# A two-layer encoder on one core: loads at the end of the recurrence move from SyncE's queue to GpSimd's

## The chip, the cores and the metric

One of the eight cores of a Trainium2 chip runs the whole program. The metric is the device time of one execution in microseconds; the time of a kernel is the median of several runs. Engines are called by name: TensorE (PE in the profile; PEld is its weight load), VectorE (DVE), ScalarE (ACT), GpSimd (POOL) and SyncE (SP). SyncE computes nothing: it issues transfers. ScalarE and GpSimd can issue transfers as well, from their own queues, between their own instructions. Each queue is worked off in order.

## The reference, cut to what matters

The model is a trunk of two layers on 768 tokens, two sequences of 512 and 256 that share the weights. In layer 0 two mixers run side by side on the normalised input, four heads of differential attention and eight heads of a bidirectional RWKV-7 recurrence, and share an output projection:

```python
st = (st * w_t[:, :, None, :] + sa[..., None] * (kk_t * a_t)[:, :, None, :]
      + v_t[..., None] * k_t[:, :, None, :])
y = jnp.einsum('bhvk,bhk->bhv', st, r_t)
...
y = ((y - mean) * lax.rsqrt(var + RWKV_GN_EPS)).reshape(B, S, H * N) * lnx_w + lnx_b
return ((y + bonus.reshape(B, S, H * N)) * g).astype(xn.dtype)
...
return jnp.concatenate([out_a.astype(xn.dtype), out_b], axis=-1) @ w_out0
```

Layer 1 is dilated window attention in three groups. Each layer ends with a SwiGLU feed-forward of width 2816, and each part has an RMS norm before and behind it. All is float32.

## The kernel before, in words

Tokens are worked on in six tiles of 128. Products with weights run in three passes: a weight or an activation is cast to a rounded upper half by ScalarE, the lower half is the difference, taken by VectorE or GpSimd (`split`, lines 137 to 140), and upper times upper, upper times lower and lower times upper are added. A weight matrix comes in blocks of 512 KB: `raw` (lines 132 to 135) takes one of two buffers `wraw` and issues its load from SyncE, `weights` splits it. The lower halves of the output projection `wo0` are taken by GpSimd.

The recurrence is worked in chunks of 64 tokens, twelve forward and twelve backward, in alternation (`rwkv`, from line 916). For each chunk `fetch` and `fetch_inverse` (lines 938 to 956) load seven pieces from device memory, all from SyncE's queue: KB, two halves of RH, AL, two halves of the values into SUV, and the inverse Ti. They are fetched three chunks ahead. RH, AL, SUV and Ti have four buffers, KB three. `prep` makes the products that need no state and `chain` does the step itself, with copies by ScalarE and VectorE between its small products. When both directions have passed both chunks of a tile, `finish` (line 1029 on) ends it: it loads the tile's values into `gz` (line 1036), which has one buffer, takes mean and variance on VectorE with a square on ScalarE into `gq`, a power on GpSimd (lines 156 and 157), then loads the tile's gate into `gq`, one buffer shared with the square (line 1044), multiplies and adds on VectorE (lines 1045 to 1050), and has TensorE transpose the result, which is split into the operand of the output projection. Two tiles end at the sixth step of the twelve, two at the eighth and two at the last.

The rounds of the recurrence are written in three parts. The first five run beside the differential attention. Then come the sixth to the ninth, after them the four raw loads of the attention's rows `o` and the eight blocks of `wo0`, and then the last three. Behind them the output projection runs over the tiles (`outproj`), each tile followed by its post-norm (`postnorm`, lines 224 to 236), which needs `mix_post` and the tile's row `x`, both loaded by SyncE into space that the recurrence gives free. The projection takes five banks in turn for its half tiles, and the post-norm frees them. Before the last two tiles `ahead` loads the first two blocks of `gate0` with `raw` and the first of `up0` with SyncE. Then the feed-forward of layer 0 starts.

The order of instructions on each engine is not the order of the program: a planner simulates time, with priorities. Rounds have a raised priority, `prep` a lowered one, and float32r products the lowest, so that they fill gaps. The program order of the loads thus says only what they depend on.

Of the kernel before, what the change touches and what calls it, by code (L numbers as in the profile page):

```python
# [18 lines left out]
P = 128  # L19
# [35 lines left out]
class Core:  # L55
# [3 lines left out]
    def __init__(self, ctx, tc, A):  # L59
        self.tc, self.nc, self.A, self.ctx = tc, tc.nc, A, ctx  # L60
        nc = self.nc
        self.n, self.half, self.turn, self.last = 0, 0, 0, None
        self.qk, self.dq, self.dv, self.banks = {}, {}, {}, {}
        self.const = ctx.enter_context(self.pool("const"))
        self.sm = ctx.enter_context(self.pool("sm", bufs=6))
        self.mh = self.const.tile([P, 8], F32, tag="mh", name="mh")
        nc.gpsimd.memset(self.mh, -0.5)
        nc.scalar.activation(out=self.small("warm", 8, 1), in_=self.mh, func=AF.Square)
# [62 lines left out]

    def raw(self, src, w=1024):
        r = self.wp.tile([P, 1024], F32, tag="wraw", name=self.uid("wraw"), bufs=self.rb)
        self.nc.sync.dma_start(r[:, :w], src)
        return r

    def split(self, hi, lo, x, eng=None):
# [164 lines left out]

    def ffn(self, L, X, hp, post, end, ready):

# [8 lines left out]
        def up(ms):  # L313
# [7 lines left out]
            def product(W, x):  # L321
                o = three(self.bank(UP)[:, 0:H])
                for k in range(4):
                    ws = slice(k * P, (k + 1) * P)
                    for j, (w, a) in enumerate(((0, 0), (0, 1), (1, 0))):
                        self.mm(o, W[w][:, ws], x[a](k), k == 0 and j == 0, k == 3 and j == 2)
                return o

            def add(o, x, b, eng=nc.vector):
                eng.tensor_tensor(out=o, in0=x, in1=b, op=ALU.add)  # L330

            def run(n):
# [8 lines left out]
                def result(i, j, f, *a):  # L341
                    o = sv[:, i, j]
                    if n == 0:
                        f(o, *a)
                        nc.scalar.activation(out=o, in_=o, func=AF.Silu)
                    else:
                        f(a[0], *a)
                        nc.gpsimd.tensor_tensor(out=o, in0=o, in1=a[0], op=ALU.mult)  # L348
                v1 = vec("v1", 2)
                nc.scalar.copy(out=v1, in_=product(next(W), X["B11"]))  # L350
                yield
                p2 = product(next(W), X["B21"])
                yield
                p4 = product(next(W), X["T4"])
                u1, u2, v5 = vec("u1"), vec("u2"), vec("v5")
                add(u1, v1, product(next(W), X["T2"]))
                result(0, 0, add, v1, p2)
                nc.scalar.copy(out=v5, in_=product(next(W), X["T1"]))
                add(u2, u1, product(next(W), X["T3"]))
# [556 lines left out]
    def rwkv(self, rw, park, out):  # L916

        nc, A = self.nc, self.A
        am = []
        for d in "fb":  # L920
            t = rw.tile([P, P], I32, tag="am" + d, name="am" + d)
# [107 lines left out]
        def finish(t):  # L1029

            y = ys[:, t]
            hv = lambda x: x.rearrange("p (h v) -> p h v", h=8)
            bc = lambda x: x.unsqueeze(2).to_broadcast([P, 8, 64])
            st = tile("gst", [P, 3, 8], 2)
            z, q = (tile(n, [P, 512]) for n in ("gz", "gq"))
            nc.sync.dma_start(z, park["v"][t * P:(t + 1) * P])
            nc.vector.tensor_reduce(out=st[:, 0], in_=hv(y), axis=AX.X, op=ALU.add)
            nc.vector.tensor_scalar(out=st[:, 0], in0=st[:, 0], scalar1=1.0 / 64, scalar2=None, op0=ALU.mult)
            nc.vector.tensor_tensor(out=hv(y), in0=hv(y), in1=bc(st[:, 0]), op=ALU.subtract)
            nc.scalar.activation(out=q, in_=y, func=AF.Square)  # L1040
            nc.vector.tensor_reduce(out=st[:, 1], in_=hv(q), axis=AX.X, op=ALU.add)
            self.rpow(st[:, 2], st[:, 1], 1.0 / 64, 64e-5)
            g = tile("gq", [P, 512])
            nc.sync.dma_start(g, park["g"][t])
            nc.vector.tensor_tensor(out=hv(z), in0=hv(z), in1=bc(self.bon[:, t]), op=ALU.mult)
            nc.vector.tensor_tensor(out=z, in0=z, in1=lb, op=ALU.add)
            nc.vector.tensor_tensor(out=hv(y), in0=hv(y), in1=bc(st[:, 2]), op=ALU.mult)
            nc.vector.tensor_tensor(out=y, in0=y, in1=lw, op=ALU.mult)
            nc.vector.tensor_tensor(out=z, in0=y, in1=z, op=ALU.add)
            nc.vector.tensor_tensor(out=z, in0=z, in1=g, op=ALU.mult)  # L1050
            b = self.bank("tr")
            for j in range(4):
                self.tr(b[:, j * P:(j + 1) * P], z[:, j * P:(j + 1) * P])
            out(t, b)
# [264 lines left out]
def body(ctx, tc, A):  # L1319
    nc = tc.nc  # L1320
    C = Core(ctx, tc, A)
    dp = ctx.enter_context(tc.tile_pool(name="dp", bufs=1, space=DRAM, reuse_waits="tile"))
    park = {}
# [64 lines left out]
    def wo(L, n, pool):  # L1388

        def slot(i):  # L1390
            return None if i < C.wb else [pool.tile([P, 1024], F32R, tag=f"{x}{i}", name=C.uid(x)) for x in ("xwh", "xwl")]
        return [C.weights(A[f"wo{L}"][i], slot=slot(i), eng=None if L else nc.gpsimd) for i in range(n)]
    extra = ExitStack()
    rounds(SW, SO)
    for j in range(4):
        C.split(xh[:, j], xl[:, j], C.raw(park["o"][j], T)[:, :T])
# [5 lines left out]
    def wides(L, pool):  # L1402
        return C.wide(pool, f"mix_post{L}", "wpost"), C.wide(pool, f"ffn_pre{L}", "wpre")

    def out_and_norm(L, src, Ws, ks, wide=None):

        sides[0] = ExitStack()
        raw = sides[0].enter_context(C.pool(f"r3{L}", side="right")).tile([P, D], F32, tag="r3", name=C.uid("r3"))
        xp = sides[0].enter_context(C.pool(f"xt{L}", side="right"))
        xt = [[xp.tile([P, 4, T // 2], F32R, tag=f"T{i}{n}", name=C.uid("T")) for n in "hl"] for i in range(3)]  # L1410
        with C.phase(f"ho{L}") as hp:
            C.tmp, C.bw = hp, D
            xs = [hp.tile([P, D], F32, tag="x", name=C.uid("x"), bufs=3) for t in range(NT)]
            wq, wr = wide or wides(L, hp)
            for t in range(NT):
                nc.sync.dma_start(xs[t], src[t])

            def done(t, ms):
                C.postnorm(ms, wq, xs[t])
                nc.sync.dma_start(park["x"][t], xs[t])  # L1420
                C.prenorm(t, xs[t], wr, xh, xl, tags=NORM, xt=xt)
            ready = []
            C.outproj(xh, xl, done, lambda: ready.extend(C.ahead(L, raw)), Ws, ks)
        extra.close()
        return operands(xt), ready
# [11 lines left out]
    def ffn(L, X, ready):  # L1437
        with C.phase(f"hf{L}") as hp:
            w, xs = {}, {}

            def fetch(t, eng):
                xs[t] = C.tmp.tile([P, D], F32, tag="xr", name=C.uid("xr"), bufs=4)
                eng.dma_start(xs[t], park["x"][t])

            def end():
                sides[0].close()
                sides[0] = ExitStack()
                C.tmp, C.bw = sides[0].enter_context(C.pool(f"end{L}", side="right")), D
                w["q"] = C.wide(C.tmp, f"ffn_post{L}", "wpost")
                if L == 0:  # L1450
                    w["r"] = C.wide(C.tmp, "mix_pre1", "wpre")

            def post(t, m):
                if t == 0:
                    for i in range(4):
                        fetch(i, nc.sync)
                x = xs[t]
                C.postnorm(m, w["q"], x, halves=L == 1 and t == NT - 1)
                if L == 1 and t == NT - 1:
                    nc.sync.dma_start(A["y"][t, :, 0:512], x[:, 0:512])  # L1460
                    nc.scalar.dma_start(A["y"][t, :, 512:D], x[:, 512:D])
                elif L == 1:
                    nc.sync.dma_start(A["y"][t], x)
                else:
                    nc.gpsimd.dma_start(park["x"][t], x)
                    if t:
                        C.prenorm(t - 1, xs[t - 1], w["r"], xh, xl, tags=("sc", "ob"))
                    if t == NT - 1:
                        C.prenorm(t, x, w["r"], xh, xl, tags=("sc", "ob"))
                if 1 <= t <= 2:  # L1470
                    fetch(t + 3, nc.sync if L else nc.gpsimd)
            C.ffn(L, X, hp, post, end, ready)
        sides[0].close()

    X = out_and_norm(0, A["x"], W, range(8))
    ffn(0, *X)
    extra = ExitStack()
    xw = extra.enter_context(C.pool("xw1"))
# [155 lines left out]
```

## Time and profile before

| | |
|---|---|
| median of 3 runs | 2126.71 us (2123.24 to 2132.2) |
| the profiled execution | 2126.21 us, span 2124.4 us |
| TensorE busy | 2048.7 us, 96% of the span |
| VectorE, ScalarE, GpSimd busy | 65%, 43%, 42% of the span |
| issues of SyncE's queue (q1) | 168.00 MB, 25.4% of the transfer engines' time |
| issues of ScalarE's (q10) and GpSimd's (q0) | 12.03 MB and 6.83 MB |
| mean granted clock of TensorE | 0.973 of full |

The span runs from the first to the last instruction. In the lists of instructions the columns are the start and the duration in us, the engine, the line of the kernel, the operation, what it writes and reads, how many were merged, and in brackets the idle time of the engine before it and what ended that. A q behind an engine's name marks its queue, as for an issue of a transfer. A stretch of time is given in us from the span's start.

### The profile page before, as it was taken

Reading aid. Unit: us, or ns where it says so; the run is one execution under the profiler, and the core shown is the slowest. Engines: PE = TensorE matmul, PEld = TensorE weight load, DVE = VectorE, ACT = ScalarE, POOL = GpSimd, SP = SyncE. Lnnn points to the kernel's source line nnn. Section 1 sums busy time; section 2 is a strip of 40 time slices with the busy share of each in tenths; the row PEclk is TensorE's granted clock in tenths of the full one; section 3 lists DMA queues with packets and bytes.
Section 4 is the critical chain, followed back from the end, with each engine's and each line's share of the span. In section 5 each row is a group of like instructions: output and inputs, shape, how many; then the busy total and the mean of one; then the engine's idle time right before and its main releaser. Section 6 shows DMA issues by size and latency. Waiting matters only on the chain. (4 is left out here: it accounts for less than half of the span.)

```text
span 2124.4 us, 33739 instructions
## 1 busy us (share of the span) xinstructions
PE 2048.7 (96%) x13270; PEld 1772.5 (83%) x13270; DVE 1378.2 (65%) x2147; ACT 905.9 (43%) x1703; POOL 886.5 (42%) x833
## 2 busy tenths in 40 slices
PE   7999999999998989999999999999998999999998
PEld 7767776777887778999999998888677999999997
DVE  5456996856579566566666657543568566666665
ACT  5467555447554254433333335222444433333332
POOL 4344341653113156543444535443137544543442
PEclk9999997999999999999999999999999999999999
DMA  4334434114365311211222235221131222221124
GB/s 156 87 75 90 97 74 137 55 26 144 84 184 161 129 64 61 80 60 60 73 77 70 72 137 193 74 71 38 51 109 60 71 79 70 70 69 60 60 80 149
DMA packets 150227, 189.01 MB, mean 89 GB/s; under 512 B 95926, under 2 KB 107784, under 8 KB 150068
## 3 DMA queue, kind: packets, MB, share of 16 engines
q1 hardware_dynamic: 126880, 168.00, 25.4%
q10 hardware_dynamic: 20372, 12.03, 2.0%
q0 software_dynamic: 2816, 6.83, 1.0%
q8 instruction: 104, 1.70, 0.3%
q14 instruction: 55, 0.45, 0.1%
HBM read 150.20 MB, written 36.23 MB: 88 GB/s over the span
## 5 line engine op out<-in xcount | busy, mean ns | idle before, releaser
L83 PE MATMUL gm<-xh,w 128*128 128x384 f32 x896 | 249.1, 342 | 2.8 <-ACT xh L139 2.8
L140 DVE TENSOR_TENSOR wl<-wraw,wh 128x1024 fp32r<-128x1024 f32 (+1 forms) x96 | 126.0, 1313 | 151.7 <-ACT wh L139 150.3
L83 PE MATMUL gm<-T,w 128*128 128x384 f32 x1032 | 203.6, 340 | 7.9 <-ACT w L139 7.3
L83 PE MATMUL gm<-xh,wh 128*128 128x256 f32 (+3 forms) x640 | 208.8, 348 | 0.8 <-ACT pad L489 0.8
L83 PE MATMUL gm<-xl,wh 128*128 128x256 f32 (+3 forms) x640 | 207.6, 348 | 0.0
L83 PE MATMUL gm<-xh,wl 128*128 128x256 f32 (+3 forms) x640 | 206.1, 346 | 0.0
L140 DVE TENSOR_TENSOR w<-S,w 128x512 fp32r<-128x512 f32 x176 | 168.8, 961 | 43.8 <-ACT w L139 36.4
L83 PEld LDWEIGHTS gm<-T,w 128*128 128x128 f32 x1032 | 184.1, 188 | 12.7 <-ACT w L139 8.5
L139 ACT CAST wh<-wraw 128x1024 fp32r<-128x1024 f32 (+1 forms) x103 | 107.5, 1046 | 163.8 <-PE gm L83 96.8
L139 ACT CAST w<-S 128x512 fp32r<-128x512 f32 x176 | 108.9, 621 | 156.7 <-POOL S L291 54.6
L83 PEld LDWEIGHTS gm<-xh,w 128*128 128x128 f32 x896 | 167.3, 192 | 7.7 <-ACT xh L139 3.6
L139 ACT CAST w<-wraw 128x512 fp32r<-128x512 f32 x126 | 76.0, 620 | 206.7 <-PE gm L83 138.1
L83 PE MATMUL gm<-xl,w 128*128 128x384 f32 x448 | 153.4, 342 | 3.0 <-DVE xl L140 3.0
L293 POOL TENSOR_TENSOR S<-wraw,S 128x512 f32<-128x512 f32 x42 | 62.8, 1496 | 204.8 <-DVE w L140 204.8
L140 DVE TENSOR_TENSOR w<-wraw,w 128x512 fp32r<-128x512 f32 x126 | 117.5, 949 | 38.1 <-ACT w L139 37.9
L83 PE MATMUL sc<-xh,w 128*128 128x384 f32 x512 | 140.8, 336 | 1.0 <-DVE u L330 1.0
L83 PEld LDWEIGHTS gm<-xh,wh 128*128 128x128 f32 (+1 forms) x640 | 120.2, 194 | 21.8 <-issue 5.8
L83 PEld LDWEIGHTS gm<-xh,wl 128*128 128x128 f32 (+1 forms) x640 | 119.9, 194 | 20.6 <-issue 7.0
L83 PEld LDWEIGHTS gm<-xl,wh 128*128 128x128 f32 (+1 forms) x640 | 120.0, 194 | 19.7 <-issue 7.3
L392 DVE TENSOR_TENSOR acc<-acc,ob 128x512 f32<-128x512 f32 x128 | 87.4, 683 | 66.6 <-PE ob L83 65.5
L83 PE MATMUL sc<-T,w 128*128 128x384 f32 x552 | 111.2, 340 | 7.4 <-ACT v L350 3.3
L348 POOL TENSOR_TENSOR sil<-sil,v 128x384 f32<-128x384 f32 x44 | 46.9, 1066 | 163.1 <-DVE v L330 162.9
(502 smaller groups left out, 5301.5 us busy)
## 6 DMA issues: line engine op xcount, KB each, us to landing
wraw<-in_gate SPq DMA_DIRECT2D x44, 512.0 KB, 3.4
wraw<-in_down SPq DMA_DIRECT2D x44, 512.0 KB, 3.7
wraw<-in_up SPq DMA_DIRECT2D x40, 512.0 KB, 3.5
wraw<-in_wqk SPq DMA_DIRECT2D x20, 512.0 KB, 3.7
wraw<-in_wo SPq DMA_DIRECT2D x14, 512.0 KB, 4.0
wraw<-in_wrkv SPq DMA_DIRECT2D x12, 512.0 KB, 3.5
KB<-pkKB SPq DMA_DIRECT2D x24, 256.0 KB, 3.2
pkx<-x SPq DMA_DIRECT2D x12, 512.0 KB, 3.4
```

Source lines behind the costliest of these rows:

```text
L83: return self.nc.tensor.matmul(o, a, b, start=start, stop=stop)
L139: self.nc.scalar.copy(out=hi, in_=x)
L140: (eng or self.nc.vector).tensor_tensor(out=lo, in0=x, in1=hi.bitcast(F32), op=ALU.subtract)
L293: eng.tensor_tensor(out=s2, in0=a12, in1=s2, op=ALU.subtract)
L348: nc.gpsimd.tensor_tensor(out=o, in0=o, in1=a[0], op=ALU.mult)
L392: nc.vector.tensor_tensor(out=accs[t][:, fs], in0=accs[t][:, fs], in1=os[t, f], op=ALU.add)
```

## The change

`raw` issues its load from `self.rq`. That is SyncE's queue, but from line 1394, between the fifth and the sixth round of the recurrence, to the feed-forward of layer 0, as the program is written, it is GpSimd's. The two loads of each tile end are issued by GpSimd always. The loads that `fetch`, `fetch_inverse`, `wides`, the rows of `x` and the direct load of `up0` issue stay with SyncE.

```diff
@@ __init__
+        self.rq = nc.sync
@@ raw
         r = self.wp.tile([P, 1024], F32, tag="wraw", name=self.uid("wraw"), bufs=self.rb)
-        self.nc.sync.dma_start(r[:, :w], src)
+        self.rq.dma_start(r[:, :w], src)
@@ finish
-            nc.sync.dma_start(z, park["v"][t * P:(t + 1) * P])
+            nc.gpsimd.dma_start(z, park["v"][t * P:(t + 1) * P])
...
-            nc.sync.dma_start(g, park["g"][t])
+            nc.gpsimd.dma_start(g, park["g"][t])
@@ body
     extra = ExitStack()
+
+    C.rq = nc.gpsimd
     rounds(SW, SO)
     for j in range(4):
         C.split(xh[:, j], xl[:, j], C.raw(park["o"][j], T)[:, :T])
...
     X = out_and_norm(0, A["x"], W, range(8))
+    C.rq = nc.sync
     ffn(0, *X)
```

## Rows read from the trace of the kernel before

**Rows 1.** The page's first part: busy us, share, instructions.

```profile
PE 2048.7 (96%) x13270; PEld 1772.5 (83%) x13270; DVE 1378.2 (65%) x2147; ACT 905.9 (43%) x1703; POOL 886.5 (42%) x833
```

**Rows 2.** Busy us by stretch: length, PE, PEld, DVE, ACT, POOL, clock, DMA share, GB/s.

```profile
600.00:685.00 85.00, 74.67 (x1262) 65.08 (x1260) 78.49 (x131) 44.66 (x95) 27.97 (x18) 1.00 0.64 190
...
720.00:740.00 20.00, 17.29 (x82) 14.20 (x81) 12.20 (x16) 10.29 (x24) 4.86 (x12) 1.00 0.74 278
```

**Rows 3.** Waits of TensorE, 600 to 740 us: total us, times, longest.

```profile
PE gm L83 <- DVE xn L233: 2.7, 1, 2.7
PE gm L84 <- DMA RH<-pkRH: 2.0, 3, 0.8
```

**Rows 4.** SyncE's issues in order of time.

```profile
652.41 0.60 SPq L952 DMA_DIRECT2D SUV<-pkv  x1
655.34 0.33 SPq L1036 DMA_DIRECT2D gz<-pkv  x1
...
656.20 1.17 SPq L948 DMA_DIRECT2D RH<-pkRH  x2
...
672.28 0.54 SPq L1036 DMA_DIRECT2D gz<-pkv  x1
674.19 0.33 SPq L1044 DMA_DIRECT2D gq<-pkg  x1
674.57 1.18 SPq L948 DMA_DIRECT2D RH<-pkRH  x2
```

**Rows 5.** TensorE in order of time, at four places.

```profile
661.50 0.68 PE L84 MATMUL gm<-RH,KB 128*128 128x128 f32 x4 [0.61 <-DMA RH<-pkRH]
...
679.08 0.68 PE L84 MATMUL gm<-RH,KB 128*128 128x128 f32 x4 [0.78 <-DMA RH<-pkRH]
...
685.56 0.50 PE L83 MATMUL gm<-wh,xh 128*128 128x512 f32 x1
...
724.02 0.50 PE L83 MATMUL gm<-wh,xh 128*128 128x512 f32 x1 [2.71 <-DVE xn L233]
```

**Rows 6.** Transfers of layer 0's end issued by GpSimd: ns, min/median/max.

```profile
L1465 POOL DMA_DIRECT2D pkx<-xr x6: 536/611/676, 1278.8 to 1310.0; - x6
```

**Rows 7.** The last lower half of `wo0`; all operations of line 1048, ns min/median/max.

```profile
665.22 2.63 POOL L140 TENSOR_TENSOR xwl<-wraw,xwh 128x1024 fp32r<-128x1024 f32 x1 [0.73 <-ACT xwh L139]
...
L1048 DVE TENSOR_TENSOR ys<-ys,lw x6: 684/692/2871, 633.2 to 713.6; 128x512 f32<-128x512 f32 x6
```

**Rows 8.** Idle time of the engines at `wraw`, 600 to 680 us: us, times.

```profile
  DMA wraw<-in_wo: 2.5, 3
  DMA wraw<-pko: 1.5, 2
```

**Rows 9.** SyncE's issues in order of time, 703 to 722 us.

```profile
704.15 7.02 SPq L1044 DMA_DIRECT2D gq<-pkg  x2
714.50 0.32 SPq L1036 DMA_DIRECT2D gz<-pkv  x1
719.32 0.33 SPq L179 DMA_DIRECT2D mix_post<-in_mix_post  x1
```

**Rows 10.** VectorE in order of time, 703 to 728 us.

```profile
708.71 0.69 DVE L1050 TENSOR_TENSOR gz<-gz,gq 128x512 f32<-128x512 f32 x1
...
717.15 0.69 DVE L1045 TENSOR_TENSOR gz<-gz,bon 128x512 f32<-128x512 f32 x1 [1.33 <-DMA gz<-pkv]
```

**Rows 11.** GpSimd in order of time, 704 to 712 us.

```profile
704.86 1.63 POOL L157 TENSOR_TENSOR gst<-var,mh 128x8 f32<-128x8 f32 x1
```

**Rows 12.** Transfers by issuer: times, KB each, median us from issue to landing.

```profile
gz<-pkv SPq DMA_DIRECT2D x6, 256.0 KB, 2.7
...
mkband<-in_mask_band POOLq DMA_DIRECT2D x1, 192.0 KB, 4.7
```

**Rows 13.** VectorE and GpSimd in order of time, 1284 to 1288 us.

```profile
1287.49 0.68 DVE L233 TENSOR_TENSOR xn<-acc,ffn_post 128x512 f32<-128x512 f32 x1
...
1287.27 0.53 POOL L1443 DMA_DIRECT2D xr<-pkx  x1 [0.65 <-DVE xn L191]
```

## The prediction

> **What bounds the kernel now.** I read the page first. TensorE is busy for 96% of the span [rows 1]: over the whole kernel there are about 76 us in which it does nothing, and a change that only moves loads can win no more than its share of these. Then I asked for the busy time in the touched stretch, the end of the recurrence and the output projection behind it. From 600 to 685 us TensorE is busy 74.67 of 85 us and VectorE 78.49; from 720 to 740 us TensorE is busy 17.29 of 20 [rows 2]. The reader is to see that TensorE idles for 10.3 us in the first stretch and 2.7 in the second, and that in the first VectorE has even less room than TensorE. The third view is TensorE's own waits [rows 3]: 2.7 us, once, for VectorE in the first post-norm, and 2.0 us, in three waits, for a transfer, the RH blocks. These are the waits that the change can touch.
>
> **The change part by part.** It moves 26 issues off SyncE's queue: 14 raw loads (four of `o`, eight of `wo0`, two of `gate0`), and the two loads `gz` and `gq` of each of six tile ends. SyncE keeps the fetches of the recurrence.
>
> *What SyncE loses.* Its queue is in order, so a load that waits holds the fetches behind it. I went through its issues in order of time [rows 4]. At 653.0 us it is through with a fetch, then stands at `gz` until 655.34 (the block is still being transposed), and reaches the next RH at 656.20. TensorE wants that RH at 660.9 and goes on 0.61 us later [rows 5]. At 672.8 it is the same: `gq` goes out at 674.19, RH at 674.57, and TensorE is 0.78 us late [rows 5]. Without the moved loads these RH leave up to 3.2 and 1.8 us earlier, more than the two waits, so both can go: 0.61 + 0.78 = 1.39 us. The third wait, the other 0.6, I leave as it is. What is late next is VectorE, busy 92% there [rows 2]: it can keep the whole gain. Bounds 0 and -1.4; I take the middle, **-0.7**.
>
> *What GpSimd gets.* A load that it issues takes 0.61 us of its time at the median [rows 6], so 26 take 16 us. Its queue is in order too: a load that waits holds what stands behind it, which is the lower halves of `wo0` and the short power of each tile end. The last half is done at 667.9 [rows 7], and the projection that needs it begins at 685.6 [rows 5], so a hold of up to 17 us there costs nothing. Beside such a half a VectorE operation is stretched: line 1048 takes 2.87 us in place of 0.69 [rows 7]. The eight halves stay and only move, since the loads of `wo0` no longer stand behind fetches; where they fall decides which step of the recurrence pays. I take 0 for it, within plus and minus 4 (two halves on or off the chain).
>
> *ScalarE's casts.* Its queue has a cast for each raw load, and between them the copies of the recurrence. It waits 2.5 us for `wo0` and 1.5 for `o` now [rows 8]. The loads leave earlier but may land later (below). If all 4.0 us were on the path and went, that would be -4; if each of twelve casts waited 2 us more, 24 us of ScalarE would go, and with ScalarE busy for half of the stretch [rows 2] the path would feel about half, +12. **0** is nearer to the rows.
>
> *The tile ends.* Four of six fall where the recurrence still has work for TensorE. The last two stand on the path, and I followed them step by step. `gz` leaves at 714.50 [rows 9] and VectorE waits for it until 717.15 [rows 10]; three operations of 0.7 us free the block into which the post-norm's weights are loaded, and `mix_post` leaves at 719.32 [rows 9]; it lands, VectorE multiplies, and TensorE, out of banks, goes on at 724.02 after 2.71 us [rows 5]. Each delay of that `gz`, or of the step before it, is paid one to one. For the first of the two, `gq` leaves at 704.15 [rows 9] and is wanted at 708.71 [rows 10]; GpSimd has the power from 704.86 to 706.49 [rows 11]. Put ahead of the power, the issue makes the power 0.6 late; put behind it, the load leaves 2.3 us later and lands 0.5 late if it takes 2.7 us, as `gz` does from SyncE [rows 12], or 2.5 late with two more. I take **+0.6**. For the second, `gz`, 256 KB, lands in 2.7 us; of GpSimd's own loads the nearest in size, 192 KB, in 4.7 [rows 12]. So 0 to 2.0; I take half, **+1.0**, as that is one load alone. Ends for both steps together: +0.5 and +4.5.
>
> The Trainium skill has a price of its own for this: DMA: Bandwidth & Descriptors, section "Latency and other measured facts", puts the first byte at some 0.6 us on SyncE's path and 1 us on GpSimd's. By that, an estimate, the second step would be +0.4 in place of +1.0 and the sum +0.3. Rows 12 show 2.0 us between two loads of nearly one size; no row here has the same load from both queues.
>
> **The sum.** -0.7 + 0 + 0 + 0.6 + 1.0 = +0.9 us. The profiled execution took 2126.21 us, 1.8 more than its span, and lies 0.5 under the median of the three runs, 2126.71. So 2127.1 for a like execution and **2127.6** for the median. About 0.5%, 10.6 us, is what a measurement of this kernel can tell from no change: the forecast is no difference that can be told.
>
> **Rivals.**
> *SyncE paced the recurrence.* For it: the two holds of rows 4. If the whole recurrence moves up, its price is TensorE's 10.3 us of idle time from 600 to 685 us: 2126.7 - 10.3 = 2116.4. Against it: only 2.0 of TensorE's waits are for a transfer [rows 3], and VectorE is nearly full.
> *GpSimd's loads land late and ScalarE holds the recurrence.* This is the one on the other side. Place: the casts of line 139 in ScalarE's queue, one for each of twelve raw loads. Price: 1 to 2 us on each, 12 to 24 us, 2139 to 2151. It decides from the point at which ScalarE's wait for raw loads, now 4.0 us [rows 8], passes some 12. For it: 4.7 against 2.7 us [rows 12]. Against it: the loads leave earlier, and half of ScalarE's time is free.
> *Issues on GpSimd and VectorE's operations shut each other out.* Twenty issues fall from 604 to 685 us; if each stretches a VectorE operation by its own 0.61 us, that is 12 us on the fullest engine: 2139. Against it: beside an issue at 1287.27 us a VectorE operation kept its 0.68 us, and the issue took 0.53 [rows 13]. The Trainium skill (SBUF — State Buffer, section "SBUF: two separate sides") has such a shut-out, for descriptors that GpSimd writes while VectorE runs a copy in a two-port mode; by that rule rows 13 prove little, since the operation there multiplies two inputs.
>
> **How the numbers follow.** Forecast 0.72, the first rival 0.10, the second 0.13, the third 0.05. The order on all engines is planned anew with the new queues, so steps that I have not named can change places; with the plus and minus 4 above I spread the forecast itself by about 7 us on either side. Slower by over 0.5% (above 2137.3): most of the second and third rivals, 0.14, and 0.03 of the forecast's edge, **0.17**. Faster by over 0.5% (under 2116.1): half of the first rival and 0.02 of the edge, **0.07**. Within: **0.76**. The range for 8 in 10 takes the forecast with its edges, most of the first rival and the near end of the other two: **2117 to 2142**.
>
> **What would show it.** In the changed kernel: RH on SyncE no longer behind `gz` and `gq`, and TensorE's waits for RH at about 0.6 us in place of 2.0; 26 more issues of about 0.6 us on GpSimd; TensorE's wait for the post-norm grown from 2.7 to about 4.3 us; ScalarE's waits for raw loads still near 4. I am wrong if the stretch from 600 to 685 us shortens or lengthens by more than 5 us, or if the time moves in a stage behind 770 us, where nothing is moved and only another order or another granted clock could do it.

## The result: 0.8% slower, and the profile after

The changed kernel takes 2143.39 us (median of 5 runs, 2140.52 to 2147.31) against 2126.71 (2123.24 to 2132.2, 5 runs beside them): a ratio of 1.0077, 95% interval 1.0054 to 1.0099, or 16.7 us slower. The forecast was no difference, 2127.6, within 2117 to 2142. The profiled execution took 2147.31 us, its span is 2145.5.

The page's busy line and the stretches that answer to [rows 1, 2], with two stretches behind the change; after each stretch come its length, then PE, PEld, DVE, ACT and POOL, the granted clock, and the transfers:

```profile
PE 2062.1 (96%) x13270; PEld 1785.5 (83%) x13270; DVE 1382.2 (64%) x2147; ACT 907.1 (42%) x1703; POOL 902.1 (42%) x859
```

```profile
600.00:685.00 85.00, 73.48 (x1118) 65.39 (x1120) 73.04 (x118) 42.24 (x87) 39.87 (x37) 0.88 0.64 186
720.00:740.00 20.00, 13.76 (x57) 10.83 (x56) 9.96 (x14) 6.10 (x15) 3.94 (x6) 0.83 0.50 180
800.00:900.00 100.00, 93.15 (x477) 88.60 (x478) 59.78 (x72) 46.85 (x81) 55.82 (x41) 0.95 0.21 69
1600.00:1700.00 100.00, 87.09 (x446) 80.53 (x445) 71.88 (x84) 49.86 (x90) 66.99 (x51) 0.93 0.20 69
```

The last two of these in the kernel before:

```profile
800.00:900.00 100.00, 95.96 (x514) 91.00 (x515) 62.85 (x77) 43.76 (x76) 59.48 (x45) 1.00 0.22 74
1600.00:1700.00 100.00, 91.84 (x494) 86.07 (x493) 68.68 (x76) 47.63 (x84) 63.14 (x46) 1.00 0.20 67
```

The reader is to see three things. The 13270 instructions that the profile counts on TensorE take 13.4 us more of busy time. From 600 to 685 us it is busy about as long as before (73.5 against 74.7) but gets 1118 instructions done in place of 1262; its clock is at the half level, 1.2 of 2.4 GHz, for some 20 of the 85 us (a mean of 0.88 against 1.00), which is 10 us of its work. And such stretches come again behind 770 us, where no load was moved. The two windows shown are those where before has none; it has its own just ahead of them (0.91 from 740 to 800 us, 0.92 from 1500 to 1600, where the changed kernel has 0.97 and 0.95), so that from 740 us to the end the half clock takes 16 us of work in before and 24 here. By the post-norm's `mix_post` the kernel is 11.4 us late (730.71 against 719.32 [rows 9]), at the end of the span 21.1.

TensorE's waits, 480 to 860 us (total us, times, longest; this kernel's lines are one higher than before's from 62 to 1394), to be read beside [rows 3]:

```profile
PE gm L84 <- DVE xn L234: 3.5, 1, 3.5
PE sc L85 <- ACT Xs L1002: 2.9, 1, 2.9
PE tr L88 <- DVE gz L1051: 2.8, 1, 2.8
PE sc L85 <- ACT SUV L997: 2.6, 1, 2.6
PE gm L85 <- DVE SUV L1009: 2.6, 1, 2.6
...
PE ob L85 <- ACT Xs L1002: 1.6, 1, 1.6
...
PE gm L85 <- DMA RH<-pkRH: 0.4, 1, 0.4
```

ScalarE's waits for raw loads, 600 to 720 us [rows 8], and its first two of them in order of time:

```profile
ACT xh L140 <- DMA wraw<-pko: 4.5, 2, 2.9
...
ACT wh L140 <- DMA wraw<-in_wo: 4.0, 3, 2.1
...
ACT xwh L140 <- DMA wraw<-in_wo: 1.3, 1, 1.3
```

```profile
608.69 0.83 ACT L140 CAST xh<-wraw 128x768 fp32r<-128x768 f32 x1 [2.92 <-DMA wraw<-pko]
609.43 0.36 ACT L1009 COPY SUV<-ob 64x256 f32<-64x256 f32 x1
611.36 0.83 ACT L140 CAST xh<-wraw 128x768 fp32r<-128x768 f32 x1 [1.57 <-DMA wraw<-pko]
612.10 0.58 ACT L986 COPY KBT<-gm 128x512 f32<-128x512 f32 x1
```

By these lines the wait for RH is down to 0.4 us, as the change intended. But the 2.6 us that are put down to VectorE's `SUV` belong to a product that reads RH and no `SUV`. Its two RH halves, issued from 644.90 on, took 6.1 and 5.7 us, beside a `wo0` block that GpSimd had issued at 644.65; the second half landed at 651.23, 0.24 us before the product starts:

```profile
644.65 0.61 POOL L135 DMA_DIRECT2D wraw<-in_wo  x1 [0.30 <-POOL wl L141]
```

```profile
644.90 1.17 SPq L949 DMA_DIRECT2D RH<-pkRH  x2
```

```profile
DMA to landing us min/median/max: 5.7/5.9/6.1
```

```profile
651.47 2.05 PE L85 MATMUL gm<-RH,KB 128*128 128x128 f32 x8 [2.58 <-DVE SUV L1009]
```

In the second profile of this kernel (`e4_after_again`) the same product waits 2.63 us, put down to yet another step of VectorE, and RH lands 0.25 us before it. So TensorE waits for RH some 3.0 us, against 2.0 before.

New are 7.1 us in which TensorE waits for ScalarE's copies, between 604 and 621 us. In ScalarE's queue the copies at 609.43 and 612.10 stand right behind casts that wait for raw loads. The copies that end TensorE's two longer waits do not: the one at 614.12 had itself waited 1.45 us for VectorE, and the one at 620.12 stood behind a square that waited for VectorE.

The tile ends, on GpSimd, VectorE and TensorE [rows 5, 10, 11], and the landing of the moved loads (KB, median us) [rows 12]:

```profile
714.56 0.57 POOL L1045 DMA_DIRECT2D gq<-pkg  x1
715.16 1.67 POOL L158 TENSOR_TENSOR gst<-var,mh 128x8 f32<-128x8 f32 x1
...
725.63 0.60 POOL L1037 DMA_DIRECT2D gz<-pkv  x1 [1.60 <-PE tr L88]
```

```profile
728.53 0.69 DVE L1046 TENSOR_TENSOR gz<-gz,bon 128x512 f32<-128x512 f32 x1 [1.86 <-DMA gz<-pkv]
```

```profile
735.65 0.80 PE L84 MATMUL gm<-wh,xh 128*128 128x512 f32 x1 [3.47 <-DVE xn L234]
```

```profile
gz<-pkv POOLq DMA_DIRECT2D x6, 256.0 KB, 3.3
```

### The profile page after: what moved, and what is told of

Read it like the earlier page. It is cut to its first block, busy times and chain, and to the rows that moved or that the text cites. A ratio compares the mean times of both kernels' runs of the same rounds, so it can differ in the third digit from the quotient of the medians.

```text
span 2145.5 us, 33781 instructions
## 1 busy us (share of the span) xinstructions
PE 2062.1 (96%) x13270; PEld 1785.5 (83%) x13270; DVE 1382.2 (64%) x2147; ACT 907.1 (42%) x1703; POOL 902.1 (42%) x859
```

## The experiments

The planner had put 742 of the 11154 instructions that the program has for TensorE in another order, and 315 on the other engines. So there were two suspects, the new queue and the new order, beside the half clock. All times are compared with runs of the kernel before on the same chip.

### The parts, planned anew, and both kernels again

`e1_ends`, the tile ends alone:

```diff
-            nc.sync.dma_start(z, park["v"][t * P:(t + 1) * P])
+            nc.gpsimd.dma_start(z, park["v"][t * P:(t + 1) * P])
...
-            nc.sync.dma_start(g, park["g"][t])
+            nc.gpsimd.dma_start(g, park["g"][t])
```

> Only the two loads gz and gq of each tile end are issued by GpSimd; the raw loads stay on SyncE. The changed kernel was 16.7 us slower. Theory A (the raw loads: ScalarE's casts wait longer for them, 9.8 us in place of 4.0, and hold the recurrence): this kernel is near the kernel before, within 3 us, 2124 to 2130. Theory B (the tile ends: gz and gq wait in GpSimd's queue and come late): most of the loss is here, 2135 to 2143, and TensorE's start of the post-norm's stretch is 5 us or more late. Theory C (the loads themselves cost little; the planner puts all engines in another order, and TensorE's clock drops to half in the gaps that this makes): the time need not follow either part, anything from 2118 to 2145, and a slower one shows more stretches at half clock from 600 us on than the 27 us of before.

Measured: 2140.84 us, ratio 1.0073 (1.0055 to 1.0091).

`e2_raws`, the raw loads alone:

```diff
...
-        self.nc.sync.dma_start(r[:, :w], src)
+        self.rq.dma_start(r[:, :w], src)
...
-    extra = ExitStack()
+    extra = ExitStack(); C.rq = nc.gpsimd
...
```

> Only the raw loads of o, wo0 and gate0 are issued by GpSimd; gz and gq stay on SyncE. Theory A (ScalarE's casts wait for the raw loads): 2137 to 2143, with ScalarE's waits for raw loads from 600 to 720 us near 10 us. Theory B (the tile ends): within 3 us of before, 2124 to 2130. Theory C (another order, and the half clock that its gaps bring): the sum of this and of the kernel with only the tile ends moved need not be the 16.7 us of the whole; anything from 2118 to 2145.

Measured: 2137.61 us, 1.0050 (1.0031 to 1.0070). Either part has most of the loss, 15.5 and 10.6 us, and they don't add up to the whole: what theory C allows, and neither A nor B.

`e3_before_again` and `e4_after_again`, no edit:

> The kernel before, profiled again, to see how much of the difference in granted clock is between executions and not between kernels. If the clock is a property of the order of the work (theory C), the stretches at half clock from 500 us on stand at the same places as in the first profile (770.7, 791.2, 1521.7, 1593.3 and the end) within a few us, some 27 us in sum, and none from 600 to 700 us. If they come and go by themselves, they stand elsewhere, and the two traces of before and after can't be compared by them.

> The changed kernel, profiled again. Theory C: the granted clock from 600 to 685 us is again near 0.88 and the stretches at half clock from 500 us on are again some 68 us in sum, at 606, 620, 651, 733 us and so on. If the clock comes and goes by itself: near 1.00 from 600 to 685 us, and the time below 2135 or the loss somewhere else.

Measured: 2124.04 and 2143.37 us. From 600 to 685 us, before and then after:

```profile
600.00:685.00 85.00, 75.74 (x1232) 66.09 (x1231) 80.26 (x134) 42.51 (x90) 28.05 (x18) 0.98 0.64 185
```

```profile
600.00:685.00 85.00, 75.53 (x1120) 67.09 (x1117) 73.67 (x122) 40.61 (x84) 38.78 (x38) 0.86 0.64 179
```

The lower clock of that stretch belongs to the kernel, not to the execution. Before is not quite free of it: one short drop, near 662 us, was not expected.

### Queue and order taken apart

`e5_after_old_order` has the new queues and the old order, `e6_before_new_order` the old queues and the new order:

```diff
             body(ctx, tc, A)
+            pin(tc)
...
+        if prev is not None:
+            tc.add_manual_dep(ins[f"I-{n}"], prev, info, reason="pin")
+        prev = f"I-{n}"
```

`pin` adds an edge that only fixes the order of issue from each instruction to the next one on its engine, in the order of the other kernel. The 26 loads are left free. The edges themselves cost nothing that shows: two kernels below that have them and move no load or only two take before's time (0.9993 and 0.9991 of it).

> The changed kernel with its queues (26 loads on GpSimd), but every other instruction of every engine held, by edges that only fix the order of issue, in the order that the kernel before has; the planner only chooses where the 26 loads stand in GpSimd's queue. Theory A/B (the loads themselves cost the time: late landing, holds in GpSimd's queue): the loss stays, 2138 to 2146, and the granted clock from 600 to 685 us is again under 0.95. Theory C (the loads cost next to nothing, the planner's new order costs it): back to the kernel before, 2122 to 2132, and the clock from 600 to 685 us is 0.98 or more.

> The reverse: the kernel before with all its loads on SyncE, but every other instruction in the order of the changed kernel. Theory A/B (the queue costs it): 2124 to 2130. Theory C (the order costs it): the loss appears without the change, 2138 to 2146, with the granted clock from 600 to 685 us under 0.92 and the first down projection's stretch (800 to 900 us) under 1.00. If both this and the run with the old order are slow, queue and order each cost a part, and the parts are read from the two.

Measured: 2140.11 us, 1.0056 (1.0037 to 1.0075), for the new queue in the old order, and 2154.68, 1.0113 (1.0097 to 1.0128), for the new order with the old queue. So both cost: the queue 11.9 us, the order 24.0. Together they cost 16.7, less than the order alone. That the new order was made for loads that come from GpSimd may be why; it was not tested. Each of the two runs an order beside queues that it was not planned for, so neither figure is a share of the 16.7. I had expected one or the other.

In `e5_after_old_order` the instructions stand in before's order, so its trace can be laid beside before's one by one. The RH product of 600 to 602 us is 5.4 us ahead of before's (a difference of the first 500 us), the post-norm's first product, 724.02 there, is 6.7 behind it: 12 us lost between. On VectorE three steps on `gz` stand out:

```profile
641.93 2.56 DVE L1045 TENSOR_TENSOR gz<-gz,bon 128x512 f32<-128x512 f32 x1 [1.93 <-DMA gz<-pkv]
...
661.78 3.60 DVE L1046 TENSOR_TENSOR gz<-gz,lb 128x512 f32<-128x512 f32 x1
681.44 0.69 DVE L1045 TENSOR_TENSOR gz<-gz,bon 128x512 f32<-128x512 f32 x1 [6.13 <-DMA gz<-pkv]
```

```profile
675.41 1.67 POOL L157 TENSOR_TENSOR gst<-var,mh 128x8 f32<-128x8 f32 x1
677.04 0.62 POOL L1036 DMA_DIRECT2D gz<-pkv  x1
```

```profile
680.63 1.13 PE L84 MATMUL gm<-RH,KB 128*128 128x128 f32 x8 [1.95 <-DMA RH<-pkRH]
```

`gz` leaves behind GpSimd's power at 677.04 (SyncE had issued it at 672.28 [rows 4]) and VectorE stands 6.13 us for it; at 675.36 in before it had waited 0.15. With the 1.93 these are 8.1 us of waits for `gz` that before does not have.

Two steps on `gz` take 2.56 and 3.60 us beside a lower half on GpSimd, but that is not new. In before two such steps are as long:

```profile
642.97 2.73 DVE L1046 TENSOR_TENSOR gz<-gz,lb 128x512 f32<-128x512 f32 x1
...
662.39 2.65 DVE L1046 TENSOR_TENSOR gz<-gz,lb 128x512 f32<-128x512 f32 x1
```

Over all steps of VectorE from 600 to 720 us, against the shortest of their line and shape and counting those of more than 0.3 us, the stretches add up to 13.8 us in before (eight steps), 13.1 in the changed kernel (seven) and 15.7 here (eight): about 2 us of the 12.

And an RH can land late when a moved load passes it. The two halves of one RH, issue to landing, first in before (issued 612.2 to 613.7) and then here (606.5 to 608.2, with a `wo0` block issued by GpSimd at 607.63, behind both):

```profile
DMA to landing us min/median/max: 2.5/2.6/2.6
```

```profile
DMA to landing us min/median/max: 2.9/4.0/5.1
```

The product that needs it waits until 612.42, 1.55 us in place of 0. TensorE's waits for an RH that had landed just before, this one among them, add up to 5.3 us here against 2.0 in before and 3.0 in its second profile. One queue is no shelter either: in before the RH of 656.20 left 0.44 us behind a `wo0` block of SyncE's own queue and took as long:

```profile
DMA to landing us min/median/max: 4.6/4.8/5.0
```

From 600 to 690 us the median RH half lands in 3.6 us here and in 3.8 in before. The Trainium skill says of this (DMA: Bandwidth & Descriptors, "Rules for kernel authors") that spreading transfers over the issuing engines gives no bandwidth, because all run on the same 16 transfer engines and interleave. The 5.1 us beside a block from the other queue and the 5.0 behind one from the same queue agree.

### The parts in the old order

`e7_ends_old_order` and `e8_raws_old_order` are `e1_ends` and `e2_raws` with `pin` and the order of before.

> Only gz and gq are issued by GpSimd, and all engines are held in the order of the kernel before. With the whole change in that order the loss was 11.4 us (2140.11 against 2128.74). In that run's trace TensorE and VectorE lose time at two kinds of place: where gz comes late or a VectorE step on gz is stretched (VectorE waits 1.9 and 6.1 us, steps of 2.56 and 3.60 us in place of 0.69), and where an RH block lands late beside a moved load. Theory 'tile ends': gz in GpSimd's queue is most of it, 6 to 10 us here, 2133 to 2138. Theory 'raw loads beside RH': 0 to 3 us here, 2127 to 2131.

> Only the raw loads are issued by GpSimd, all engines in the order of the kernel before. Theory 'raw loads beside RH': the raw loads pass the fetches, RH lands 5 us after its issue in place of 2.6 and TensorE waits for it: 4 to 9 us, 2132 to 2137. Theory 'tile ends': 0 to 4 us, 2127 to 2132. If the two parts are independent, this loss and that of the tile ends alone add up to about 11 us.

Measured: 2135.04, 1.0024 (1.0010 to 1.0038), and 2132.72, 1.0013 (1.0001 to 1.0025): 5.1 and 2.8 us. Each part costs less than its own theory wanted (6 to 10 and 4 to 9), and the two make 8 of the 11.9, which the intervals don't tell from all of it. Planned anew the same two had cost 15.5 and 10.6: there the order takes 10 and 8 us, and the intervals don't touch.

`e9_gz_first` is `e5_after_old_order` with the 26 loads held too, and two `gz` put earlier in GpSimd's queue: one ahead of a lower half of `wo0`, one ahead of a power's two steps. The edit is only in the list that `pin` reads.

> The whole change in the old order, but in GpSimd's queue two gz stand earlier: the third tile end's ahead of a lower half of wo0, the fifth's ahead of a power's two steps. In the run without this VectorE waited 1.9 and 6.1 us for these two. If the in-order hold in GpSimd's queue costs what the waits show: 4 to 7 us faster than that run, 2133 to 2137. If the transfers beside each other cost it (gz then lands as late, or the RH beside it later): the same, 2138 to 2142.

Measured: 2139.13, 1.0053 (1.0035 to 1.0070): no gain that can be told from 2140.11. VectorE's wait of 6.13 us is 0.72 now, but another step on `gz` falls beside a lower half and takes 4.38 us:

```profile
647.87 4.38 DVE L1046 TENSOR_TENSOR gz<-gz,lb 128x512 f32<-128x512 f32 x1
...
682.00 0.69 DVE L1045 TENSOR_TENSOR gz<-gz,bon 128x512 f32<-128x512 f32 x1 [0.72 <-DMA gz<-pkv]
```

In all, VectorE's stretches grow only from 15.7 to 16.9 us. The medians show no gain; the intervals, 7.5 to 14.9 us of loss against 7.9 to 16.0, leave room for one of several us. The traces do show one, in one profile each. From the RH product that stands at 601.07 in before to the projection's first product at 685.56 [rows 5], in the same order on TensorE, it takes 84.5 us in before (84.4 in its second profile), 95.9 in `e5_after_old_order`, 88.9 in `e9_gz_first`, 95.5 with the tile ends alone and 88.5 with the raw loads alone. So in the traces the tile ends make most of the loss in this stretch, and the two waits for `gz` some 7 us of it. That the medians of `e9_gz_first` and of the tile ends alone (5.1) do not follow stays open.

`e10_gz_two_buffers`, old queues, old order, a second buffer for `gz`:

```diff
-            z, q = (tile(n, [P, 512]) for n in ("gz", "gq"))
+            z, q = tile("gz", [P, 512], 2), tile("gq", [P, 512])
```

> No load is moved to GpSimd: all stay on SyncE, all engines in the old order, and gz has two buffers, so that its load need not wait until the block before it is transposed, and holds no RH behind it. This takes away what the change wanted to take away, without the other queue. If SyncE's holds at gz cost what the first prediction read from the kernel before (1.4 us of TensorE's waits for RH, and the last gz 2 us earlier at the tail): 2 to 4 us faster than the kernel before. If an earlier gz only moves the transfers' collision with RH to another place: no difference, within 2 us.

Measured: 2126.88, 0.9993 (0.9980 to 1.0005). What the change was to relieve, SyncE held at `gz`, is worth nothing that can be measured (4 us faster to 1 us slower).

### Is it the order?

`e12_gz_two_buffers_replanned` is the last kernel without `pin`.

> Two buffers for gz, all loads on SyncE, and the planner free to order all engines anew. Held in the old order this was no slower than before (2126.88 against 2129.08), so what differs here is the order alone; against the order of before it puts 262 of TensorE's 11154 instructions out of place. Theory 'the planner's new order is bad because it plans for GpSimd's loads': within 3 us of that, 2124 to 2131. Theory 'the order of before is a lucky one, and any new plan loses': 5 us slower or more, 2132 to 2142.

Measured: 2129.74, 1.0008 (0.9994 to 1.0021). A new plan need not lose, so the theory that any new plan loses falls. But this order also lies nearer to before's, with 262 of TensorE's instructions out of place against 742 in the changed kernel and 555 in the next one, which both lose. Whether the distance decides, whatever queue the plan is for, was not tested.

`e13_first_end_replanned` moves 2 of the 26 loads, planned anew; `e16_first_end_old_order` holds the same in before's order; `e17_before_first_end_order` has the order of the first and no load moved (in the last two the other 24 loads are held too):

```diff
-            nc.sync.dma_start(z, park["v"][t * P:(t + 1) * P])
+            ends[0] += 1; lq = nc.gpsimd if ends[0] == 1 else nc.sync; lq.dma_start(z, park["v"][t * P:(t + 1) * P])
...
-            nc.sync.dma_start(g, park["g"][t])
+            lq.dma_start(g, park["g"][t])
```

> Of the 26 moved loads only two, gz and gq of the first tile end, are issued by GpSimd, and the planner is free; TensorE has 555 instructions out of place against before. Two loads that wait for nothing but themselves can cost at most some 3 us by the queue (1 to 2 us of late landing each). Theory 'order': the loss is nevertheless near that of all loads, 6 to 16 us, 2134 to 2144. Theory 'queue': 0 to 3 us, 2126 to 2131.

> Only gz and gq of the first tile end are issued by GpSimd, as in the run that was planned anew and took 2140.06 (13 us more than before), but all engines are held in the order of the kernel before. Theory 'order': the two loads by themselves cost 0 to 3 us, 2126 to 2131. Theory 'queue': the loss stays, 2136 to 2143.

> The reverse: all loads on SyncE, every engine in the order that the planner made for the kernel with the two loads of the first tile end on GpSimd. Theory 'order': the loss is here without any load moved, 2135 to 2145. Theory 'queue': 2126 to 2131.

Measured: 2140.06, 1.0056 (1.0036 to 1.0076); 2127.05, 0.9991 (0.9975 to 1.0008); 2154.33, 1.0122 (1.0096 to 1.0148). By themselves the two loads cost nothing that can be measured; the order that the planner makes for them costs 12 us with them and 26 without. From 600 to 685 us in these three:

```profile
600.00:685.00 85.00, 74.57 (x1068) 64.87 (x1066) 70.63 (x117) 40.62 (x83) 28.42 (x19) 0.88 0.61 180
```

```profile
600.00:685.00 85.00, 77.91 (x1259) 68.57 (x1259) 76.53 (x130) 43.72 (x92) 29.12 (x19) 0.94 0.65 190
```

```profile
600.00:685.00 85.00, 69.88 (x938) 60.67 (x936) 64.20 (x103) 37.00 (x79) 26.85 (x19) 0.82 0.59 170
```

The old order gets 1259 instructions of TensorE done, the new one 1068 and 938. One thing that it does on TensorE, in `e13_first_end_replanned`: a transpose of the attention's rows stands in its queue before VectorE has made them, and the recurrence stands behind it. In before no wait as long falls there. It is under 3 of the 12 us; the rest was not traced.

```profile
598.62 0.69 PE L87 MATMUL tr<-ident,o 128*128 128x128 f32 x2 [2.75 <-DVE o L901]
```

### Is it the half clock?

`e11_after_filled`, `e14_after_filled_more` and `e15_before_filled` put products of the identity with itself in front of instructions for which TensorE waits:

```diff
+        for _ in range(FILL.get(key, 0)):
+            self.mm(o, self.ident, self.ident)
```

> The changed kernel in its own order, with 28 extra products of the identity with itself put on TensorE in front of the five instructions for which it waits longest between 600 and 655 us (4, 8, 6, 2 and 8 of them, some 0.28 us each at full clock), into banks that the next product overwrites. They add 7.8 us of TensorE's work to stretches in which it stands still, and take nothing off the waits. Theory 'half clock': the drops at 606, 620 and 651 us (20.4 us at half, 10 us of work) follow from TensorE standing still, and cost beyond the waits: the granted clock from 600 to 685 us rises from 0.88 to 0.95 or more and the time falls by 4 to 10 us, 2133 to 2139. Theory 'waits alone': the chain over ScalarE and VectorE sets the pace whatever the clock is: 2141 to 2147, the clock up or not.

> The changed kernel in its own order, with 94 extra products of the identity with itself on TensorE, in front of 17 instructions for which it stands still in both profiles of the changed kernel, from the recurrence's end to the first third of each layer's feed-forward (1 to 11 of them, 0.28 us each at full clock, as many as fit the shorter of the two waits). The waits stay; 26 us of TensorE's work is added to them. In the run with 28 such products the profiled execution had lost 1.4 us to the half clock from 600 to 700 us in place of 10.2 and took 2128 us, but the median was 2143.7. Theory 'half clock costs two thirds of the loss': median 2128 to 2138 and a mean granted clock of 0.970 or more in place of 0.967. Theory 'the clock only goes along with the waits': 2141 to 2150.

> The same with the kernel before, in its own order: 64 extra products in front of 11 instructions of TensorE that wait in both of its profiles (two in the recurrence, the first post-norm, and those around 769 to 827 and 1593 to 1623 us). Before loses 5.2 to 6.8 us to the half clock from 700 to 800 us and 8.5 from 1500 to 1700. Theory 'half clock': 2 to 8 us faster than before, 2119 to 2125, which would beat both kernels. Otherwise the same or slower by what the extra products delay, 2126 to 2133.

Measured: 2143.68, 1.0063 (1.0044 to 1.0082); 2143.07, 1.0071 (1.0055 to 1.0086); 2128.2, 0.9995 (0.9985 to 1.0005). The profiled execution of the first took 2128 us, which looked like the proof; but its first 500 us, where nothing was filled, ran at 0.95 where after's ran at 0.91, and 16.9 of its 19 us were won there. With 94 products the clock did rise, from 0.967 to 0.972 over the runs, and in the profile from 0.88 to 0.94 and from 0.93 to 0.98:

```profile
600.00:685.00 85.00, 75.14 (x1184) 67.25 (x1179) 71.37 (x120) 42.50 (x90) 39.45 (x37) 0.94 0.66 186
...
1600.00:1700.00 100.00, 88.43 (x480) 82.08 (x479) 72.26 (x84) 50.05 (x90) 68.13 (x52) 0.98 0.21 69
```

The time did not follow. The extra products are more work than the clock gave back, 26 us against some 16 (the half clock's share of each stretch behind 500 us, added up and compared with both profiles of the changed kernel), so this does not settle whether the half clock costs by itself; it does show that filling the waits is no remedy. `e16_first_end_old_order` says more: its clock from 600 to 685 us is 0.94 too, 5 us of work, and between the two products named above it takes 84.1 us, no more than the 84.5 of before at 1.00. So half clock in this stretch need not cost anything.

## Why the prediction was wrong

- **SyncE's relief, -0.7 us.** This did not come true: TensorE's waits for RH are some 3.0 us, against 2.0 [rows 3], the longest for an RH that took 6.1 us to land beside a `wo0` block. I had read the RH of 656.20 as late by the hold alone; it had also taken 5.0 us to land. `e10_gz_two_buffers`, which only takes the holds at `gz` away, shows no gain, though its interval can't tell 0.7 us from none.
- **GpSimd's issues, 16 us of its time.** Right: 902.1 against 886.5 busy [rows 1], 15.6.
- **The lower halves, "I take 0 for it, within plus and minus 4".** Right: VectorE's steps are stretched by 13.1 us in all against 13.8, and by 15.7 in the old order.
- **ScalarE's casts, 0.** Mis-sized: the waits for raw loads grew from 4.0 to 9.8 us, short of the 12 that I had set as the point of the second rival. The raw loads alone cost 2.8 us (0.2 to 5.3) in the old order; how much of that goes through the casts was not measured.
- **The last two tile ends, +0.6 and +1.0.** Close: the issue of `gq` puts the power 0.60 late (714.56, 715.16); from the last `gz`'s issue to VectorE it is 2.90 us against 2.65 [rows 9, 10], +0.25, and to TensorE's post-norm 10.02 against 9.52, +0.5. By the first-byte times of the Trainium skill (DMA: Bandwidth & Descriptors, "Latency and other measured facts") my estimate for that `gz` was +0.4, nearer than my 1.0.
- **"Four of six fall where the recurrence still has work for TensorE."** This failed first. It put the other four tile ends at nothing, and `e5_after_old_order` measures +11.9 (7.9 to 16.0) in an unchanged order, where my sum was +0.9. The tile ends alone cost 5.1 (2.1 to 8.1) there, where I had +1.6 for them. TensorE had work, but VectorE, the fullest engine of that stretch [rows 2], takes its steps in order and stood 8.1 us for two `gz` that had left behind GpSimd's own steps. The raw loads, at 0 in my sum, cost the 2.8, with RH landing late beside them. That the waits for `gz` are the cause is what the traces say; the medians of `e9_gz_first` do not confirm it.
- **"The order on all engines is planned anew ... I spread the forecast itself by about 7 us on either side."** This failed second: a spread about zero, where the measured shifts are +10, +8 and +14 us for the three parts (`e1_ends`, `e2_raws`, `e13_first_end_replanned`, each against its run in the old order). For the whole change it is +4.5, which its intervals don't tell from zero.
- **The test I had set** was met on both counts: the recurrence's last step on VectorE starts 9.7 us later (711.18 against 701.45), of which some 2 were there before 600 us already, and some 9.5 us were lost behind the post-norm's start, where only order and clock differ.

By the runs' own means, time multiplied by granted clock is 2067 us for before (27 runs, clock 0.972) and 2072 for after (5 runs, 0.967): at one clock the loss would be 5 us, and the other 11 go with the lower clock. That is arithmetic: with the 94 extra products the clock was 0.972, as in before, and the time still 2143. Whether the clock is the cause of any of it stays open, as does why the planner's orders for loads on GpSimd are worse than its order for SyncE.

## What to carry to other kernels

Where a planner orders the engines, the queue of two loads can re-order hundreds of instructions: hold the old order and run the change, then run the new order without the change, before any wait is blamed. Ask of every step that waits for a moved load which engine stands for it, and not only whether TensorE has other work. A bulky load in a second queue can leave beside a small urgent one that it used to follow, and slow it; behind a bulky load of its own queue the small one was as slow. And an idle queue on an engine that computes is not idle for loads: they wait for its work, and its work for them.

## What the runs showed of the hardware

- Transfers in flight together slow each other, from two queues or from one: half an RH block landed in 2.6 us, in 5.1 and 6.1 beside a 512 KB block from GpSimd, and in 5.0 behind one from its own queue.
- A 128x512 step of VectorE on `gz` took 0.69 us alone and 2.56, 3.60 and 4.38 beside a lower half on GpSimd (2.73 and 2.65 in the kernel before).
- The clock is not only a property of a kernel: the 27 runs of before that stood beside one group of experiments ranged from 2118 us at 0.976 to 2134 at 0.969. In `e11_after_filled` 16.9 of one profile's 19 us came from a stretch that no one had touched.
